# Two FFN f-tiles column by column, six late token tiles, and the token sums in the third f-tile

## The chip, the cores and the metric

One core of one Trainium2 chip runs the whole program in one launch. The metric is the device time of one execution in microseconds (us), the median of several runs. TensorE (PE) multiplies matrices and transposes, VectorE (DVE), ScalarE (ACT) and GpSimd (POOL) do the elementwise work, and SyncE (SP) issues nearly all DMA transfers, in the order of its queue.

## The reference

Two layers of a streaming encoder over 1024 prompt tokens and 8 x 16 sample tokens (1152 rows of 1024 channels, float32). Layer 0 mixes tokens with a gated recurrence and an attention, layer 1 with trailing pooling windows. Each mixer is followed by a layer norm, a convolutional FFN and another layer norm. The change touches the FFN's first half and the end of the mixers:

```
x = layer_norm(alpha * x + mixer(x))
a, b = split(x @ w_up)                 # w_up: 1024 x 5632, so a and b have 2816 columns each
c = conv_b + a[t-2]*cw[0] + a[t-1]*cw[1] + a[t]*cw[2]
f = (silu(c) * b) @ w_down
x = layer_norm(alpha * x + f)
```

## The kernel before

**Layout.** Tokens are held in nine tiles of 128 rows (`acc`, after the layer norm) and, transposed, as channels by tokens in `xh` and `xl`: each float32 value is split into a rounded high part and the rest, and every product is three matmuls (high x high, high x low, low x high; `mm3`, L145). `to_xt` (L201) transposes one token tile: twice four transpositions on PE into a PSUM bank, then `split`: ACT copies the high part into `xh`, DVE subtracts and writes `xl`. Weights come by DMA into a `raw` tile (three buffers) and are split in halves by `split_half` (L161): ACT writes `hi`, POOL writes `lo` (eight buffers each). `load_up` loads 128 columns of `w_up` and takes two of each.

**Before the FFN.** In layer 0 the output projection (L1170 on) adds its products tile by tile to `acc`, and `layer_norm` works on each: sums and small steps on DVE, square and scaling on ACT, the gain on DVE (POOL for tiles 4, 5 and 7), the bias on POOL (L232), then a store of the rows. Three tiles later (`LATE = 3`, L1178) the tile is transposed. In layer 1 the pooling mixer does the same (L1638). The last three tiles are `late`: they are transposed inside the FFN.

**The FFN's first half** (`ffn_up`, L1190) runs over 22 f-tiles of 128 columns of a and of b. The first three (`PLAIN = 3`) are plain: six products each, part a or b times a column of 384 tokens (`CHUNKS`), 24 matmuls a product. `put_a` (ACT) copies a into `ext`, DVE copies b into `bb` (two buffers each). `conv` (L1215) turns them into `cv`: a scaling on ACT, four multiply-adds on DVE (L1225), SiLU on ACT, two small copies on POOL, the product with `bb` on DVE (L1230), a DMA to `g_scr`. The other 19 f-tiles use a recombination with seven products of half the tokens and half the channels instead of eight (`SEVEN`); it needs sums of token halves (`t1`, `t2`, `t3`, and `t4`) and sums of weights (`prepare`, L1320). One such f-tile is 168 matmuls of 288 columns. The sums of weights use the temporaries `sa` and `sb`, one buffer each, that the token sums use too.

**The token sums** (`combine`, L1276) go by four channel pairs kk. Each takes three sums on POOL (L1281, L1282, L1291), five on DVE and the splits of t1, t2, t3 (ACT, DVE). The fourth sum is split into two `raw` buffers and written to `t4_scr` in DRAM; `swap` (L1299) reads it back over the part of `xh` and `xl` that is no longer needed, since the sixth product of every recombined f-tile takes it from there. `combine` stands beside the second and the third f-tile, two steps after each product of the second, one after each of the third; `swap` stands after the third.

**Order.** The program names for each operation its engine, and a planner orders every engine's queue by its own estimates: whatever is ready by these, earliest in the program first. So an operation can be moved ahead of others that stand earlier, and on the chip each queue is then worked off in that fixed order.

Of the kernel before, what the change touches and what calls it, by code (L numbers as in the profile page):

```python
# [25 lines left out]
NT = NTOK // 128  # L26
# [15 lines left out]
LEVELS = (1, 2, 4, 8, 16, 32, 64)  # L42
LAST = 3
LATE = 3

FAST = (6, 7, 8)
PG = (1, 2, 8)
# [63 lines left out]
def hybrid_stream_kernel(ctx: ExitStack, tc: tile.TileContext, i, o, k):  # L111
# [27 lines left out]
    def bank(shape, name):  # L139
        return ps.tile(shape, F32, tag="b", name=name)  # L140
# [4 lines left out]
    def mm3(out, ah, al, bh, bl, first, last):  # L145

        mm(out, ah, bh, first, False)
        mm(out, ah, bl, False, False)
        mm(out, al, bh, False, last)
# [10 lines left out]

    def split_half(src, sub=None):  # L161

        hi = wp.tile([128, 512], F32R, tag="wh", name="hi", bufs=8)
        lo = wp.tile([128, 512], F32R, tag="wl", name="lo", bufs=8)
        split(hi, lo, src, sub or nc.gpsimd)
        return hi, lo

# [33 lines left out]
    def to_xt(src, t0):  # L201
        for j in range(0, KD, 4):
            p = bank([128, 4, 128], "pxt")
            for q in range(4):
                tr(p[:, q, :], src[:, (j + q) * 128:(j + q + 1) * 128])
            split(xh[:, j:j + 4, t0:t0 + 128], xl[:, j:j + 4, t0:t0 + 128], p)
# [35 lines left out]
    def ln_apply():  # L242
        while ln_due:
            ln_due.pop(0)()
# [850 lines left out]
    with ExitStack() as ph:  # L1095
        so = pool_of(ph, "so", 2, side="right")
        rms_scale(ssa.rearrange("p t h -> p (t h)"), 128)

        def fetch(t):
            if t not in early:  # L1100
                ot = so.tile([128, 8, 128], F32, tag="ot", name="ot", bufs=3)
                load_heads(t, ot)
                early[t] = ot, gate(t, so.tile([128, H, 128], F32, tag="gate", name="gt"))

        def heads_norm(t):
            ot, gt = early.pop(t)
            for h in range(H):
                nc.vector.scalar_tensor_tensor(ot[:, h, :], ot[:, h, :], ssa[:, t, h:h + 1], gt[:, h, :],
                                               ALU.mult, ALU.mult)
            return ot.rearrange("t h c -> t (h c)")  # L1110

        y0 = [raw_tile("y0").rearrange("p (t c) -> p t c", c=256) for _ in range(2)]

        w1 = []

        def first_columns():

            ots = {}
            for t in range(NPT + 3):
                if t == 4:  # L1120
                    w1.append(load_cols(w_out, 256))
                if t < NPT:
                    fetch(t)
                if 1 <= t <= NPT:
                    ots[t - 1] = heads_norm(t - 1)
                    yield
                if 2 <= t < NPT + 2:
                    to_xt(ots.pop(t - 2), (t - 2) * 128)
                    yield
                if t >= 3:  # L1130
                    p = bank([128, 256], "po")
                    for _ in tm_unit(w0, t - 3, p):
                        yield
                    nc.scalar.copy(y0[(t - 3) // 4][:, (t - 3) % 4, :], p)
                    yield

        weave(first_columns(), running, R5)
        last_gate = gate(NPT, so.tile([128, H, 128], F32, tag="gate", name="gt"))
        drain(running)
        at_s.close()  # L1140
        acc = open_acc()
        load_acc(acc, x_rows)
        sp = pool_of(ph, "sp", 2, side="right")
        sums = sp.tile([128, NT, 4], F32, name="sums", bufs=1)

        def out_unit(w, t, j):
            p = bank([128, 256], "po")
            drain(tm_unit(w, t, p))
            add_res(acc[t], slice(256 * j, 256 * j + 256), p, sums[:, t, j:j + 1])

        last_ot = so.tile([128, 8, 128], F32, tag="ot", name="ot", bufs=3)
        load_heads(NPT, last_ot)
        early[NPT] = last_ot, last_gate
        last_ot = heads_norm(NPT)
        for t in range(NT):
            if t == 4:
                to_xt(last_ot, NPT * 128)
            if t == 6:
                out_unit(w0, NPT, 0)
                w2 = load_cols(w_out, 512)  # L1160
            out_unit(w1[0], t, 1)
            if t < NPT:
                add_res(acc[t], slice(0, 256), y0[t // 4][:, t % 4, :], sums[:, t, 0:1])
        w3 = load_cols(w_out, 768)
        g_bc = bcast(sp, i["ln1_g"][0], "g", "g_bc")
        b_bc = bcast(sp, i["ln1_b"][0], "bb", "b_bc")
        for t in range(3):
            out_unit(w2, t, 2)
        for t in range(NT):
            if t + 3 < NT:  # L1170
                out_unit(w2, t + 3, 2)
            if t + 3 == NT - 1:
                first = [load_up(0, 0, nc.vector), load_up(0, FF, nc.vector)]
            ln_apply()
            out_unit(w3, t, 3)
            nc.vector.tensor_tensor(sums[:, t, 0:2], sums[:, t, 0:2], sums[:, t, 2:4], ALU.add)
            layer_norm(sp, acc[t], sums[:, t], g_bc, b_bc, nc.gpsimd if t in OG else None, scr_rows(0, t))
            if t >= LATE:  # L1178
                to_xt(acc[t - LATE], (t - LATE) * 128)


    HALF = NTOK // 2
# [7 lines left out]
    def ffn_up(l, acc, late, first, leave):  # L1190
# [41 lines left out]
            yield  # L1232
            nc.sync.dma_start(g_scr[l][f], cv)

        def plain(f, w, order):

            _, _, bb = begin(f)
            for part, c in order:
                a, n = CHUNKS[c]
                p = bank([128, n], "pu")  # L1240
                for kk in range(KD):
                    mm3(p, w[part][0][kk], w[part][1][kk], xh[:, kk, a:a + n], xl[:, kk, a:a + n],
                        kk == 0, kk == KD - 1)
                if part == 0:
                    put_a(f, a, p, n)
                else:
                    nc.vector.tensor_copy(bb[:, a:a + n], p)
                yield


        u = plain(0, first, [(0, 0), (0, 1), (1, 0), (1, 1), (0, 2), (1, 2)])
        for s in range(6):
            next(u)
            if s == 0:
                ln_apply()
            if s == 1:
                store_rows()
            if s in (1, 2, 3) and late:
                t = late.pop(0)
                to_xt(acc[t], t * 128)  # L1260
            if s == 3:
                second = [load_up(l, 128), load_up(l, FF + 128)]
        drain(u)
        close_acc()

        tt_s = ExitStack()
# [9 lines left out]
        def combine(kk):  # L1276
# [13 lines left out]
            A, B = temp("sa"), temp("sb")  # L1290
            nc.gpsimd.tensor_tensor(A, xh[:, 4 + kk, h0], xl[:, 4 + kk, h0], ALU.add)  # L1291
            nc.vector.tensor_tensor(B, A, C, ALU.subtract)
            parts = [raw_tile("t4") for _ in range(2)]
            split(*[r[:, 0:HALF].bitcast(F32R) for r in parts], B)
            yield
            for n in range(2):
                nc.sync.dma_start(t4_scr[l][kk, n], parts[n][:, 0:HALF])

        def swap():  # L1299
            for n, x in enumerate((xh, xl)):  # L1300
# [36 lines left out]
                   "s3": b[:, up], "s4": a[:, lo]}[name]  # L1337
            wts[n] = [x.rearrange("p (k c) -> p k c", c=128) for x in split_half(src)]

        both = [(p, c) for p in range(2) for c in range(3)]  # L1340
        side = chain(*[combine(kk) for kk in range(4)])
        third = []
        for f, w in ((1, second), (2, third)):
            u = plain(f, w, both)
            cv = conv(f - 1)
            for s in range(6):
                next(u)
                if s in (0, 2):
                    next(cv, None)
                if f == 1 and s == 4:  # L1350
                    third += [load_up(l, 256), load_up(l, FF + 256)]
                if f == 2 and s in (1, 2):
                    fetch(PLAIN, s - 1)
                if f == 2 and s >= 4:
                    prepare(s - 4)
                for _ in range(2 if f == 1 else 1):
                    next(side, None)
            drain(u)
            drain(cv)
        drain(side)  # L1360
        swap()
        fetch(PLAIN + 1, 0)
        for n in range(2, AHEAD):
            prepare(n)

        banks = {}
# [3 lines left out]
        for n in range(n_last + 1):  # L1370
            f, m = PLAIN + n // 7, n % 7
            if m == 0:
                begin(f)
            prepare(n + AHEAD)
            if m == 0 and f + 1 < NF:
                fetch(f + 1, 1)
            if m == 2 and f + 2 < NF:
# [173 lines left out]
    def pool_mixer(acc, late, ws):  # L1551

        with ExitStack() as ph:
# [61 lines left out]
            for n in range(NT + 1):  # L1615
# [19 lines left out]
                    windows(0, [(band[:, 0], us[0])])  # L1635
                elif 1 < n <= NPT:
                    windows(n - 1, [(band[:, 1], us[n - 1]), (band[:, 2], us[n - 2])])
                if n > LATE:  # L1638
                    to_xt(acc[n - 1 - LATE], (n - 1 - LATE) * 128)
            windows(NPT, [(band_s[:, 0], us[NT]), (band_s[0:120, 1], us[NPT])])  # L1640
        return first

# [2 lines left out]
    def ahead_weights():  # L1645
        got["ws"] = load_pool_weights()

    acc = conv_ffn(0, False, acc, list(range(NT - LATE, NT)), first, ahead_weights)
    first = pool_mixer(acc, list(range(NT - LATE, NT)), got["ws"])
    conv_ffn(1, True, acc, list(range(NT - LATE, NT)), first)  # L1650


_INS = ["x_prompt", "x_sample", "cache_k", "cache_v", "state_hgrn", "state_pool", "state_ffn_conv",
# [30 lines left out]
```

## Time and profile before

| | us |
|---|---|
| median of 3 runs | 2605.75 |
| lowest, highest | 2600.84, 2606.06 |
| profiled execution, its own time | 2601.48 |
| span of the profiled execution | 2599.7 |

The profile shows one execution. Its page gives each engine's busy time; the trace behind it can be asked for waits (who waited, for which operation), for a timeline of single instructions, for groups of equal instructions and for busy times in a stretch. A matmul's duration includes its way through the array; the distance from one start to the next is what a matmul costs in a row of them. The granted clock is a share of TensorE's full 2.4 GHz.

The FFN of layer 0 begins at 900.1 us, that of layer 1 at 1782.9 with three matmuls and at 1786.1 without a break.

### The profile page before, as it was taken

The numbers are of one execution on the slowest core, as the hardware profiler recorded it, in microseconds if no ns is written. First come the engines' busy times: TensorE is split into PE (matmuls) and PEld (weight loads), VectorE is DVE, ScalarE is ACT, GpSimd is POOL, SyncE is SP. The second block draws the span as 40 slices with busy tenths as digits, with TensorE's granted clock in tenths as the row PEclk, the third lists the DMA queues.
The fourth block names the chain that finished last, engine by engine and source line by source line (L and its number), as shares of the span: only waits on it lengthen the run. The fifth ranks groups of instructions, "written<-read, shape, count | busy, mean of one in ns | idle before, by whom it ended". The sixth has DMA issues, their size and how long they took to land. (4 is left out here: it accounts for less than half of the span.)

```text
span 2599.7 us, 45443 instructions
## 1 busy us (share of the span) xinstructions
PE 2505.4 (96%) x18090; PEld 2301.7 (89%) x18090; DVE 1531.6 (59%) x2706; ACT 1074.1 (41%) x2176; POOL 967.1 (37%) x729
## 2 busy tenths in 40 slices
PE   8999999999999898999999999988899999999997
PEld 8999988786879898999999788878899999987886
DVE  3377754337884675554444665787655554556557
ACT  2255545354772433444444111265344444431113
POOL 1110111005652355555554122244555555531222
PEclk9999999998999999999999999999999999999999
DMA  5744247777666114222224422222332222252222
GB/s 169 203 113 125 83 158 241 237 249 226 235 219 233 66 70 135 71 77 77 77 77 150 141 95 78 76 80 75 118 102 70 73 73 77 77 210 90 95 78 82
DMA packets 279538, 323.78 MB, mean 125 GB/s; under 512 B 46379, under 2 KB 209780, under 8 KB 279327
## 3 DMA queue, kind: packets, MB, share of 16 engines
q1 hardware_dynamic: 276901, 319.26, 37.4%
q8 instruction: 142, 2.33, 0.4%
q10 hardware_dynamic: 2426, 1.63, 0.3%
q14 instruction: 69, 0.57, 0.1%
HBM read 244.38 MB, written 76.46 MB: 123 GB/s over the span
## 5 line engine op out<-in xcount | busy, mean ns | idle before, releaser
L156 POOL TENSOR_TENSOR lo<-raw,hi 128x512 fp32r<-128x512 f32 x362 | 531.6, 1481 | 1103.2 <-ACT hi L155 976.1
L143 PE MATMUL pu<-xh,lo 128*128 128x288 f32 (+1 forms) x1504 | 457.1, 304 | 7.7 <-POOL lo L156 7.7
L155 ACT CAST hi<-raw 128x512 fp32r<-128x512 f32 x378 | 230.1, 620 | 556.7 <-PE pu L143 283.0
L143 PE MATMUL pu<-xl,hi 128*128 128x288 f32 (+1 forms) x1504 | 456.5, 304 | 3.0 <-DVE xl L156 3.0
L143 PE MATMUL pu<-xh,hi 128*128 128x288 f32 (+1 forms) x1504 | 457.1, 304 | 1.0 <-ACT hi L155 0.5
L143 PE MATMUL pd<-lo,gh 128*128 128x512 f32 x792 | 315.2, 398 | 0.0
L143 PE MATMUL pd<-hi,gh 128*128 128x512 f32 x792 | 313.7, 396 | 0.0
L143 PE MATMUL pd<-hi,gl 128*128 128x512 f32 x792 | 310.4, 393 | 0.4 <-DVE gl L156 0.4
L143 PEld LDWEIGHTS pu<-xh,lo 128*128 128x128 f32 x1504 | 283.8, 189 | 9.0 <-POOL lo L156 9.0
L143 PEld LDWEIGHTS pu<-xl,hi 128*128 128x128 f32 x1504 | 284.2, 189 | 3.6 <-DVE xl L156 3.6
L143 PEld LDWEIGHTS pu<-xh,hi 128*128 128x128 f32 x1504 | 283.9, 189 | 2.1 <-ACT hi L155 1.2
L1452 DVE TENSOR_TENSOR acc<-acc,pd 128x512 f32<-128x512 f32 x330 | 216.3, 684 | 117.5 <-PE pd L143 117.2
L143 PE MATMUL ptm<-hi,xh 128*128 128x256 f32 x720 | 209.2, 291 | 3.9 <-ACT hi L155 3.9
L1225 DVE SCALAR_TENSOR_TENSOR cv<-ext,prm,cv 128x1024 f32<-128x1024 f32 (+1 forms) x176 | 183.8, 1099 | 34.8 <-ACT cv L1222 34.8
L143 PE MATMUL ptm<-lo,xh 128*128 128x256 f32 x720 | 201.8, 280 | 0.1
L143 PE MATMUL ptm<-hi,xl 128*128 128x256 f32 x720 | 201.6, 280 | 0.0
L143 PEld LDWEIGHTS pd<-hi,gh 128*128 128x128 f32 x792 | 148.7, 188 | 38.0 <-ACT gh L155 0.6
L143 PEld LDWEIGHTS pd<-hi,gl 128*128 128x128 f32 x792 | 148.5, 188 | 36.7 <-DVE gl L156 1.3
L143 PEld LDWEIGHTS pd<-lo,gh 128*128 128x128 f32 x792 | 148.7, 188 | 33.8
L143 PEld LDWEIGHTS ptm<-hi,xh 128*128 128x128 f32 x720 | 136.3, 189 | 7.1 <-ACT hi L155 4.3
L143 PEld LDWEIGHTS ptm<-lo,xh 128*128 128x128 f32 x720 | 136.3, 189 | 0.9 <-DVE lo L156 0.4
L143 PEld LDWEIGHTS ptm<-hi,xl 128*128 128x128 f32 x720 | 135.8, 189 | 0.0
(331 smaller groups left out, 5749.4 us busy)
## 6 DMA issues: line engine op xcount, KB each, us to landing
raw<-in_ffn_w_up SPq DMA_DIRECT2D x88, 512.0 KB
kraw<-in_cache_k SPq DMA_DIRECT2D x64, 512.0 KB
vraw<-in_cache_v SPq DMA_DIRECT2D x64, 512.0 KB
g_scr<-cv SPq DMA_DIRECT2D x44, 576.0 KB
graw<-g_scr SPq DMA_DIRECT2D x44, 576.0 KB
raw<-in_ffn_w_down SPq DMA_DIRECT2D x44, 512.0 KB
raw<-in_w_in_ab SPq DMA_DIRECT2D x28, 512.0 KB
x_scr<-acc SPq DMA_DIRECT2D x18, 512.0 KB
```

What stands on the lines that cost most here:

```text
L143: nc.tensor.matmul(out, a, b, start=start, stop=stop, skip_group_check=True)
L155: nc.scalar.copy(hi, src)
L156: (sub or nc.vector).tensor_tensor(lo, src, hi, ALU.subtract)
L1225: nc.vector.scalar_tensor_tensor(dst, tap[j], cw[j], dst, ALU.mult, ALU.add)
L1452: nc.vector.tensor_tensor(acc[t][:, cs], acc[t][:, cs], p, ALU.add)
```

## The change

`LATE_UP = 6`: before the FFN only tiles 0, 1 and 2 are transposed, six tiles after they were made, and the FFN gets six late tiles. (Between layer 0 and the pooling mixer it stays at three.) The first two f-tiles are done together: for each column of tokens the four products of both, with one late tile transposed after each of the second to eighth (the fifth left out). The weights of the second f-tile are loaded after two products, those of the third after all twelve. The convolution of the first f-tile begins in the last column. The token sums: two steps before the third f-tile, three after each of its products. The fourth sum is split in two halves of 288 tokens by `split_half`, so on POOL instead of DVE and into the buffers of the weights' parts instead of `raw`, and written by four DMAs instead of two. The first weights are prepared after the fourth product of the third f-tile, and `swap` stands in the third recombined product.

```diff
-            if t >= LATE:
-                to_xt(acc[t - LATE], (t - LATE) * 128)
+            if t >= LATE_UP:
+                to_xt(acc[t - LATE_UP], (t - LATE_UP) * 128)
...
-        u = plain(0, first, [(0, 0), (0, 1), (1, 0), (1, 1), (0, 2), (1, 2)])
-        for s in range(6):
-            next(u)
-            if s == 0:
-                ln_apply()
-            if s == 1:
+        begin(0)
+        begin(1)
+        for c in range(3):
+            for f, part in ((0, 0), (0, 1), (1, 0), (1, 1)):
+                if c == 0 and f == 1 and part == 0:
+                    second = [load_up(l, 128), load_up(l, FF + 128)]
+                plain(f, second if f else first, part, c)
+                if c == 0:
+                    ln_apply()
+                if c < 2 and (f, part) != (0, 0) and late:
+                    t = late.pop(0)
+                    to_xt(acc[t], t * 128)
+                if c == 2 and f:
+                    next(cv)
+            if c == 0:
                 store_rows()
-            if s in (1, 2, 3) and late:
-                t = late.pop(0)
-                to_xt(acc[t], t * 128)
-            if s == 3:
-                second = [load_up(l, 128), load_up(l, FF + 128)]
-        drain(u)
+            if c == 1:
+                cv = conv(0)
+        third = [load_up(l, 256), load_up(l, FF + 256)]
         close_acc()
...
-            parts = [raw_tile("t4") for _ in range(2)]
-            split(*[r[:, 0:HALF].bitcast(F32R) for r in parts], B)
+            for a in (0, HALF // 2):
+                cs = slice(a, a + HALF // 2)
+                parts = split_half(B[:, cs])
+                for n in range(2):
+                    nc.sync.dma_start(t4_scr[l][kk, n][:, cs], parts[n].bitcast(F32))
             yield
-            for n in range(2):
-                nc.sync.dma_start(t4_scr[l][kk, n], parts[n][:, 0:HALF])
...
-        third = []
-        for f, w in ((1, second), (2, third)):
-            u = plain(f, w, both)
-            cv = conv(f - 1)
-            for s in range(6):
-                next(u)
...
-                for _ in range(2 if f == 1 else 1):
-                    next(side, None)
+        for _ in range(2):
+            next(side)
+        cv = chain(cv, conv(1))
+        begin(2)
+        for s in range(6):
+            plain(2, third, s // 3, s % 3)
+            for _ in range(2 if s < 4 else 1):
+                next(cv, None)
+            if s in (0, 1):
+                fetch(PLAIN, s)
+            if s >= 3:
+                prepare(s - 3)
+            for _ in range(3):
+                next(side, None)
         drain(side)
-        swap()
+        drain(cv)
         fetch(PLAIN + 1, 0)
-        for n in range(2, AHEAD):
+        for n in range(3, AHEAD):
             prepare(n)
...
             prepare(n + AHEAD)
+            if n == 2:
+                swap()
...
-                if n > LATE:
-                    to_xt(acc[n - 1 - LATE], (n - 1 - LATE) * 128)
+                if n > LATE_UP:
+                    to_xt(acc[n - 1 - LATE_UP], (n - 1 - LATE_UP) * 128)
```

## Rows read from the trace of the kernel before

**Rows 1.** Page, first part: busy us (share of the span) and instructions by engine.
```profile
PE 2505.4 (96%) x18090; PEld 2301.7 (89%) x18090; DVE 1531.6 (59%) x2706; ACT 1074.1 (41%) x2176; POOL 967.1 (37%) x729
```

**Rows 2.** TensorE's waits, 887 to 1010: waiter <- releaser: total us, times, longest.
```profile
PE pu L143 <- ACT ext L1392: 8.3, 2, 7.1
PE pxt L152 <- POOL acc L232: 5.4, 2, 5.3
PE pu L143 <- POOL lo L156: 3.9, 2, 3.1
PE pu L143 <- DVE xl L156: 3.0, 2, 1.5
```

**Rows 3.** The same, 1786 to 1892 (layer 1): the longest.
```profile
PE pu L143 <- ACT ext L1392: 7.8, 2, 6.7
```

**Rows 4.** TensorE, one line's range, and timeline: start, us, engine, line, op, tiles, [idle before].
```profile
L143 PE MATMUL pu<-xh,hi x1504: 293/296/522, 900.1 to 2304.1; 128*128 128x288 f32 x152, 128*128 128x384 f32 x36
...
922.19 1.03 PE L152 MATMUL pxt<-ident,acc 128*128 128x128 f32 x8
923.46 0.79 PE L143 MATMUL pu<-xh,hi 128*128 128x384 f32 x3 [0.24 <-ACT xh L155]
...
1004.87 0.40 PE L143 MATMUL pu<-t2h,hi 128*128 128x288 f32 x1 [1.22 <-ACT ext L1392]
...
1786.08 0.34 PE L143 MATMUL pu<-xh,hi 128*128 128x384 f32 x1
...
1887.68 0.61 PE L143 MATMUL pu<-t2h,hi 128*128 128x288 f32 x1 [1.07 <-ACT ext L1392]
```

**Rows 5.** Stretches: from:to length, busy us (count) by engine, PEclk, DMA share, GB/s.
```profile
887.00:900.00 13.00, 7.56 (x46) 7.16 (x46) 8.79 (x19) 8.15 (x14) 9.47 (x4) 0.74 0.22 77
...
923.40:956.70 33.30, 33.24 (x192) 33.24 (x192) 25.90 (x33) 14.35 (x25) 16.25 (x13) 1.00 0.26 86
...
924.20:978.20 54.00, 49.88 (x285) 48.92 (x284) 43.05 (x53) 20.56 (x33) 29.45 (x20) 1.00 0.19 64
...
1006.00:1028.00 22.00, 22.00 (x168) 22.00 (x167) 11.69 (x18) 9.81 (x20) 13.29 (x10) 1.00 0.29 92
...
1887.60:1890.00 2.40, 2.32 (x9) 2.32 (x10) 2.23 (x1) 1.44 (x5) 2.40 (x2) 0.50 0.78 238
```

**Rows 6.** POOL by group, 924.2 to 978.2: busy us, mean ns of one, idle before.
```profile
L1291 POOL TENSOR_TENSOR sa<-xh,xl 128x576 f32<-128x576 f32 x4 | 7.2, 1807 | 11.5 <-DVE sc L1285 6.4 <-DVE t1l L156 5.0
...
L1281 POOL TENSOR_TENSOR sb<-xh,xl 128x576 f32<-128x576 f32 x4 | 6.7, 1677 | 9.9 <-DVE xl L156 5.2 <-DVE t L156 4.7
```

**Rows 7.** DVE by group, the same stretch.
```profile
L1225 DVE SCALAR_TENSOR_TENSOR cv<-ext,prm,cv 128x1024 f32<-128x1024 f32 x4 | 8.0, 2002 | 0.0
...
L1284 DVE TENSOR_TENSOR sb<-sc,sb 128x576 f32<-128x576 f32 x4 | 3.0, 756 | 0.2
...
L1230 DVE TENSOR_TENSOR cv<-cv,bb 128x1152 f32<-128x1152 f32 x1 | 1.4, 1350 | 0.0
```

**Rows 8.** Timeline, POOL and DVE, single operations of the sums.
```profile
939.25 1.43 POOL L1281 TENSOR_TENSOR sb<-xh,xl 128x576 f32<-128x576 f32 x1 [4.02 <-DVE t L156]
...
957.39 1.27 POOL L156 TENSOR_TENSOR lo<-raw,hi 128x512 fp32r<-128x512 f32 x1
...
957.46 1.81 DVE L1292 TENSOR_TENSOR sb<-sa,sc 128x576 f32<-128x576 f32 x1 [1.32 <-POOL sa L1291]
```

**Rows 9.** Timeline, DVE and POOL: splits of late tiles, layer norm of tile 8.
```profile
909.34 0.68 DVE L156 TENSOR_TENSOR xl<-pxt,xh 128x512 fp32r<-128x512 f32 x1
...
915.34 2.40 POOL L232 TENSOR_TENSOR acc<-acc,b_bc 128x1024 f32<-128x1024 f32 x1
...
923.44 1.29 DVE L156 TENSOR_TENSOR xl<-pxt,xh 128x512 fp32r<-128x512 f32 x2 [0.35 <-ACT xh L155]
```

**Rows 10.** Timeline, SP's queue.
```profile
980.80 16.11 SPq L1315 DMA_DIRECT2D raw<-in_ffn_w_up  x2
996.97 0.57 SPq L1301 DMA_DIRECT2D xl<-t_scr  x1
```

More of the change, by code (lines that the diff above doesn't have):

```diff
@@ L44 @@
 LATE = 3
+LATE_UP = 6
 FAST = (6, 7, 8)
@@ L161, in split_half @@
     def split_half(src, sub=None):
-        hi = wp.tile([128, 512], F32R, tag="wh", name="hi", bufs=8)
-        lo = wp.tile([128, 512], F32R, tag="wl", name="lo", bufs=8)
+        n = src.shape[1]
+        hi = wp.tile([128, 512], F32R, tag="wh", name="hi", bufs=8)[:, 0:n]
+        lo = wp.tile([128, 512], F32R, tag="wl", name="lo", bufs=8)[:, 0:n]
         split(hi, lo, src, sub or nc.gpsimd)
@@ L1233, in conv, with plain @@
             nc.sync.dma_start(g_scr[l][f], cv)
[L1235 to L1248, printed above, removed]
-        u = plain(0, first, [(0, 0), (0, 1), (1, 0), (1, 1), (0, 2), (1, 2)])
-        for s in range(6):
-            next(u)
-            if s == 0:
-                ln_apply()
-            if s == 1:
-                store_rows()
-            if s in (1, 2, 3) and late:
-                t = late.pop(0)
-                to_xt(acc[t], t * 128)
-            if s == 3:
-                second = [load_up(l, 128), load_up(l, FF + 128)]
-        drain(u)
+        def plain(f, w, part, c):
+            a, n = CHUNKS[c]
+            p = bank([128, n], "pu")
+            for kk in range(KD):
+                mm3(p, w[part][0][kk], w[part][1][kk], xh[:, kk, a:a + n], xl[:, kk, a:a + n],
+                    kk == 0, kk == KD - 1)
+            if part == 0:
+                put_a(f, a, p, n)
+            else:
+                nc.vector.tensor_copy(open_f[f][2][:, a:a + n], p)
+        begin(0)
[13 more added lines that the diff above has]
+            if c == 0:
+                store_rows()
+            if c == 1:
+                cv = conv(0)
+        third = [load_up(l, 256), load_up(l, FF + 256)]
         close_acc()
@@ L1338, in prepare @@
             wts[n] = [x.rearrange("p (k c) -> p k c", c=128) for x in split_half(src)]
-        both = [(p, c) for p in range(2) for c in range(3)]
         side = chain(*[combine(kk) for kk in range(4)])
-        third = []
-        for f, w in ((1, second), (2, third)):
-            u = plain(f, w, both)
-            cv = conv(f - 1)
-            for s in range(6):
-                next(u)
[L1348 to L1355, printed above, removed]
-                for _ in range(2 if f == 1 else 1):
-                    next(side, None)
-            drain(u)
-            drain(cv)
+        for _ in range(2):
[12 more added lines that the diff above has]
+                next(side, None)
         drain(side)
-        swap()
+        drain(cv)
         fetch(PLAIN + 1, 0)
-        for n in range(2, AHEAD):
+        for n in range(3, AHEAD):
             prepare(n)
@@ L1646, in ahead_weights @@
         got["ws"] = load_pool_weights()
-    acc = conv_ffn(0, False, acc, list(range(NT - LATE, NT)), first, ahead_weights)
+    acc = conv_ffn(0, False, acc, list(range(NT - LATE_UP, NT)), first, ahead_weights)
     first = pool_mixer(acc, list(range(NT - LATE, NT)), got["ws"])
-    conv_ffn(1, True, acc, list(range(NT - LATE, NT)), first)
+    conv_ffn(1, True, acc, list(range(NT - LATE_UP, NT)), first)
 _INS = ["x_prompt", "x_sample", "cache_k", "cache_v", "state_hgrn", "state_pool", "state_ffn_conv",
```

## The prediction, made before the changed kernel was run

> **What bounds the kernel now.** I read the page's first part, then TensorE's waits, then the timelines and busy times of the stretches around them. TensorE is busy for 2505.4 of 2599.7 us [rows 1], so outside its waits nothing else can cost time, and the change adds or removes no matrix product and no transposition: it moves them. What it can win or lose is TensorE's idle time and the half clock behind it, in the first three f-tiles of each layer's FFN and in the stage before. There, in layer 0, TensorE waits 5.4 us for GpSimd's layer-norm addition before a transposition (the long one 5.3), 3.0 for a late xl, 3.9 for the lo parts of the third f-tile's weights and 8.3 for ext, the copy that the third recombined product has to wait for [rows 2]; in layer 1 the lo parts cost the same again and ext 7.8 [rows 3]. After such a wait the clock is lower: 0.74 of full on average over the 13 us around the layer-norm wait, 0.50 behind the ext wait of layer 1 [rows 5], which is the 1.2 GHz level.
>
> All but the first and second have one cause, and the reader can see it in one stretch. From 924.2 to 978.2 the token sums are made: DVE is busy 43.05 us and POOL 29.45, together 72.5 in 54.0 [rows 5]. They don't overlap, they block each other: a lo on POOL that began at 957.39 and takes 1.27 let DVE's sum of 957.46 end only after 1.81, against 0.756 for its equals [rows 7, 8]; POOL's sums take 1.43 alone and 1.68 to 1.81 on average here [rows 6, 8]. For operations with two SBUF inputs the two engines are one, and this one is full for the 54 us.
>
> The Trainium skill says the same in "SBUF — State Buffer", Who interferes with whom: a DVE instruction with two SBUF inputs and a GpSimd instruction that reads SBUF exclude each other for the whole instruction. The rows agree (1.81 for 0.756), and it speaks against this change, which moves a split from DVE to GpSimd inside a full stretch. By the opposite view (two free engines) the sums would hide and the first rival's time would come out.
>
> **The change part by part.**
>
> *Six late tiles, layer 0.* The wait of 5.4 us before the transposition of tile 4 goes, with about 2 us of half clock, and three tiles' transpositions (0.8 us each: eight at 922.19, then the product can go) leave the stage. The first FFN product, at 900.1 before [rows 4], could start near 890. But now tile 2 is transposed last, directly before the first column that needs it, and its splits sit where tile 5's did: between layer-norm steps of ACT and DVE. Tile 5's last xl began at 909.34 [rows 9], 10 us after its transpositions, which stood directly before the 900.1. So the first product can't end before about 900, as if it had started at S = 896; bounds 890 and 900, and I take 896 because the layer-norm chain (tile 8's last addition on POOL runs from 915.34 [rows 9]) is bound by DVE and POOL, not by the products.
>
> *Column order.* Column 0 now has four products. One product is 24 matmuls; 192 took 33.3 us [rows 5], so 4.16 each and 33.3 for the eight products of columns 0 and 1. The 3.0 us for a late xl go, as tiles 3 to 5 are wanted 17 us later. A column boundary costs 0.5 us (transposition at 922.19, product at 923.46, of which 0.8 is the transposition [rows 4]); there is one more of them per layer. The second f-tile's weights are now wanted after two products instead of six. Their lo parts go through POOL between the layer-norm additions, which run to 917.7; wanted at about 905, I take W = 2 us of waiting, bounds 0 and 8. In layer 1 these additions are further along when the FFN starts, and I take 0.
>
> *When the sums can begin.* The sums need all tokens. The last xl splits run from 923.44 for 1.29 [rows 9], 2.5 us after tile 8's transpositions began. Tile 8 is now transposed after eight products and five other late tiles instead of four and two: S + 33.3 + 5 x 0.8 + 0.5 + W + 2.5 = S + 40.3 + W. Layer 0: 938.3, against 924.7 before. Layer 1: S was 1786.1 [rows 4], less 0.5 for three matmuls that ran ahead and 0.8 for transpositions that leave the pooling stage (they partly fill its own waits, so not all 2.4): 1825.3. I call this point A.
>
> *What DVE and POOL must do from A until the second recombined product (s3) can run.* Before, four channel pairs' sums, nearly two convolutions and the four lo of the third weights took 54.0. Now: the same 54.0; less 0.75 (the first sum can run before A); less 4 x 0.75, the fourth sum's lo on DVE; plus eight of these on POOL with 288 columns, 0.72 each by 1.27 for 512 and 1.43 for 576 [rows 8]: 5.8; plus the rest of the second convolution, 1.4 for its product with bb [rows 7]; plus the first weights' lo, 1.3; plus, for s3, whose two temporaries are those of the token sums, three sums of 0.75 and one lo: 3.5. Sum 62.2. Bounds: 57 if the second convolution falls behind the sums, 67 with gaps such as ACT's part of a split.
>
> *What TensorE has from A on.* It began column 2 1.3 us before A. Four products are 16.7, the third f-tile 25.0, the first recombined product 3.1 (168 matmuls take 22.0 [rows 5], 24 of them per product): s3 is wanted at A + 43.6. It waits 18.6 us. Then 3.1 for s3 and 1.5 for the half clock, so that the third recombined product (s2) starts at A + 66.9.
>
> *What goes.* The wait for the third weights (3.9 per layer) goes: they are loaded before the third f-tile, and their buffers are free after the second column-2 product. The late raw loads go too, as the fourth sum no longer takes raw's three buffers. Both only let TensorE arrive earlier at the sums. The fourth sum's write and the exchange (SP's two reads of t4, at 996.97 before [rows 10]) stand behind the last sum at about A + 60, wanted by the sixth product at A + 76: hidden, unless something is queued before them (third rival). The halved t4 writes are four per channel pair instead of two on SP's queue, which is idle there: no cost.
>
> *The sum.* Before, s2's second half ran from 1004.87 at full clock and from 1887.68 at half [rows 4, 5], which puts s2's start at 1003.4 and, with 0.9 of lost clock, 1887.0. After: 938.3 + 66.9 = 1005.2 and 1825.3 + 66.9 = 1892.2. That is 1.8 and 5.2 later, 7.0 in all. From there both kernels run the same products. Against the profiled execution's 2601.48 us: 2608.5. That execution lies at the low end of the runs shown (2600.84, 2605.75, 2606.06), so I set the sum on the middle of low and high, 2603.5: **2610 us**.
>
> **The rivals.**
>
> *The sums hide.* If DVE and POOL work beside each other and a channel pair's chain follows the products, s2 starts at A + 46.7: 985.0 and 1872.0, 33 us earlier in all, 2570. For it: the waits named go, and TensorE has 42 us of products beside the sums. Against it: 54.0 us for the same sums in the trace, with blocked operations.
>
> *An early start and an order that favours the sums.* S = 890 and W = 0 in layer 0, and the second convolution behind the sums (57 instead of 62): s2 at 992.2 and 1887.2, 11 us earlier, 2592. For it: the layer-norm wait of 5.4 us certainly goes, and each engine's order is set by a planner that may see this. Against: tile 2's splits in the layer-norm chain.
>
> *The exchange comes late.* On SP the read of the fifth f-tile's second weights may be queued before the two reads of t4; it waits for a raw buffer that the sixth weights' split frees, at about A + 70. Two reads of 1152 KB at the 238 GB/s of this stretch [rows 5] take 10 us, so t4 lands at A + 81 instead of before A + 76: 5 us more per layer, 2620, slower. It decides from the point where the exchange is issued later than A + 66. For it: before the change just such a read stood ahead of the exchange, for 16 us [rows 10]. Against: the exchange is now behind fewer loads.
>
> **How the numbers follow.** Forecast 0.46, sums hide 0.14, early start 0.22, exchange late 0.18. About 0.2% (5.2 us around 2605.75) is what a measurement of this kernel can tell from no change. Faster (under 2600.5): all of the first rival, 0.19 of the second, 0.03 of the forecast's lower end: 0.36. Within: 0.23 of the forecast and 0.03 of the second: 0.26. Slower: 0.20 of the forecast and 0.18: 0.38. The forecast's own range is 2600 to 2621 (S 890 to 900, W 0 to 8, 57 to 67); the range for 8 in 10 reaches down past the second rival and up past the third, 2586 to 2625, and leaves out most of the first.
>
> **What would show it.** Right: no wait of TensorE for a layer-norm addition at 890 and none for the third weights; tile 8's xl about 14 and 19 us later than before; one wait of some 15 to 20 us in each layer before the second recombined product, ended by POOL's lo or DVE; DVE and POOL adding up to the stretch. Wrong: sums that end less than 50 us after tile 8's xl, or a third f-tile followed by its first products without a wait.

## The result, and the profile after

The changed kernel takes 2622.76 us (median of 4 runs, 2620.02 to 2623.65) against 2605.69 for the kernel before, also 4 runs on the same chip: a ratio of 1.0068, 95% interval 1.0051 to 1.0085. It is slower by 0.7%. The profiled execution took 2620.02, its span 2618.2, which is 18.5 more than the span before. The forecast was 2610: the right side, the right place, and less than half of the size (7.0 us, where the spans differ by 18.5 and the medians by 17.1).

Line numbers in the changed file are up to 8 higher than before. Page, first part, answering to [rows 1]: TensorE's busy time has grown by 4.5 us, with the same number of instructions: some of them ran at a lower clock.

```profile
PE 2509.9 (96%) x18090; PEld 2304.4 (88%) x18090; DVE 1545.0 (59%) x2698; ACT 1075.4 (41%) x2184; POOL 967.9 (37%) x745
```

TensorE's waits in the changed kernel, first from 880 to 1020 (layer 0, to be held against [rows 2]), behind the dots from 1770 to 1910 (layer 1, [rows 3]): total us, times, longest.

```profile
PE pu L144 <- ACT hi L156: 14.8, 2, 9.4
PE pu L144 <- ACT xh L156: 10.8, 3, 10.3
PE pu L144 <- POOL lo L157: 3.5, 2, 3.0
...
PE pu L144 <- ACT hi L156: 13.8, 2, 8.3
PE pu L144 <- POOL lo L157: 3.5, 2, 3.0
```

The waits for the layer-norm addition, for the xl, for the third weights' lo and for ext are gone. In their place stand 10.3 us for tile 2's xh in layer 0 and, in both layers, some 18 us for the parts of recombined weights. TensorE's timeline shows where, in layer 0 (start, us, engine, line, what, idle before).

```profile
890.14 1.03 PE L153 MATMUL pxt<-ident,acc 128*128 128x128 f32 x8
901.50 1.01 PE L144 MATMUL pu<-xh,hi 128*128 128x384 f32 x2 [10.32 <-ACT xh L156]
...
989.98 0.61 PE L144 MATMUL pu<-xh,hi 128*128 128x288 f32 x1 [5.41 <-ACT hi L156]
993.85 0.61 PE L144 MATMUL pu<-xh,lo 128*128 128x288 f32 x1 [3.02 <-POOL lo L157]
...
1007.84 0.61 PE L144 MATMUL pu<-t3h,hi 128*128 128x288 f32 x1 [9.43 <-ACT hi L156]
...
1009.60 0.44 PE L144 MATMUL pu<-t3h,hi 128*128 128x288 f32 x1
...
1014.37 0.29 PE L144 MATMUL pu<-t2h,hi 128*128 128x288 f32 x1
```

The first product begins at 901.50, the first recombined product waits twice, s3 begins at 1007.84, and s2 at 1014.37. Until shortly before its end, s3's matmuls are 0.24 us apart, those of s2 behind it about 0.13. The kernel before began s2 earlier than the 1003.4 that the prediction gives:

```profile
1000.44 0.61 PE L143 MATMUL pu<-t2h,hi 128*128 128x288 f32 x1 [7.12 <-ACT ext L1392]
```

But there the first half of s2 ran with its matmuls 0.24 us apart, and the second waited again [rows 4]. 1003.4 is the start from which s2 at full clock would have ended at the same time, so 11.0 us are lost up to here. The busy times of three stretches of the changed kernel show s3's half clock (length, busy us by engine in the order of [rows 5], PEclk, DMA share, GB/s; the second is from the end of tile 8's last xl, point A, to s3).

```profile
901.50:905.00 3.50, 3.50 (x13) 3.40 (x14) 2.52 (x7) 3.09 (x5) 3.37 (x3) 0.53 0.37 150
...
943.90:1007.80 63.90, 46.09 (x259) 45.19 (x257) 49.17 (x57) 24.32 (x44) 39.19 (x31) 0.86 0.21 73
...
1007.80:1014.30 6.50, 5.96 (x24) 5.62 (x25) 4.32 (x5) 3.49 (x8) 6.43 (x5) 0.52 0.50 175
```

DVE and POOL together are "busy" for 88.4 us in 63.9. Two engines that run side by side could be that busy. Here much of it is not work: an instruction that stands blocked counts as busy. The timeline of DVE and POOL in the changed kernel shows one such place; the same three multiply-adds of the convolution took 2.75 us where POOL had nothing to do (they are shown below, in the run before_dve).

```profile
942.63 1.29 DVE L157 TENSOR_TENSOR xl<-pxt,xh 128x512 fp32r<-128x512 f32 x2 [0.50 <-ACT xh L156]
...
954.71 1.88 POOL L1287 TENSOR_TENSOR sc<-xh,xl 128x576 f32<-128x576 f32 x1
...
955.22 5.99 DVE L1227 SCALAR_TENSOR_TENSOR cv<-ext,prm,cv 128x1024 f32<-128x1024 f32 x3
...
956.55 3.58 POOL L157 TENSOR_TENSOR lo<-raw,hi 128x512 fp32r<-128x512 f32 x2
```

5.99 us for 2.75 of work, beside a sum of 1.88 for 1.43 and two lo of 1.27 that took 3.58. Over the whole stretch I put each duration against that of the same instruction unblocked: by this estimate some 22 of the 88.4 us are standing still, and the 66 that are left are about as long as the stretch. At least one of the two engines is busy in 62.4 of the 63.9 us. The Trainium skill ("SBUF — State Buffer", Who interferes with whom) adds that the issue order decides which of the two engines blocks. The row agrees as far as it goes, since here both were held up in turn.

### The profile page after: what moved, and what is told of

Read it like the earlier page. It is cut to its first block, busy times and chain, and to the rows that moved or that the text cites. A ratio compares the mean times of both kernels' runs of the same rounds, so it can differ in the third digit from the quotient of the medians.

```text
span 2618.2 us, 45508 instructions
## 1 busy us (share of the span) xinstructions
PE 2509.9 (96%) x18090; PEld 2304.4 (88%) x18090; DVE 1545.0 (59%) x2698; ACT 1075.4 (41%) x2184; POOL 967.9 (37%) x745
## 5 line engine op out<-in xcount | busy, mean ns | idle before, releaser
L157 POOL TENSOR_TENSOR lo<-raw,hi 128x512 fp32r<-128x512 f32 x362 | 515.0, 1436 | 1077.7 <-ACT hi L156 951.6
```

The costliest lines, as they stand in the source:

```text
L157: (sub or nc.vector).tensor_tensor(lo, src, hi, ALU.subtract)
```

## The experiments

Every time is the median of its runs, every ratio that of its runs to runs of the kernel before on the same chip (2604.5 to 2605.9), with its 95% interval. Point A and the start of s3 are read from the timelines of DVE and TensorE.

| run | us | ratio | A, layer 0 | s3 begins | A to s3, layer 0 and 1 |
|---|---|---|---|---|---|
| the change | 2622.8 | 1.0068 | 943.9 | 1007.8 | 63.9, 63.9 |
| early3 | 2625.3 | 1.0078 | 943.9 | 1007.8 | 63.9, 63.9 |
| early_t8 | 2609.4 | 1.0017 | 933.8 | 997.7 | 63.9, 63.9 |
| late3 | 2603.3 | 0.9999 | 925.5 | 997.7 | 72.2, 72.2 |
| no_taps | 2607.2 | one run | 943.1 | 997.7 | 54.6, 54.6 |
| dve_sums | 2603.2 | 0.9993 | 942.4 | 998.8 | 56.4, 56.5 |
| early_t8_dve | 2596.6 | 0.9970 | 939.4 | 995.7 | 56.3, 56.3 |
| late3_dve | 2587.1 | 0.9933 | 924.5 | 988.5 | 63.9, 64.6 |

My theory was that A plus a fixed length of work on two engines that exclude each other sets s3, whatever TensorE does. The rivals: DVE and POOL run side by side and something else is late; the sums are a chain of operations that wait for each other, with free engines in between; or A's place doesn't matter.

### Fewer late tiles: late3

```diff
-LATE_UP = 6
+LATE_UP = 3
```

> The changed kernel with three late tiles instead of six (LATE_UP = 3), all else as changed: tile 8 is transposed after four products instead of eight. My theory (DVE and POOL are one resource for the token sums, which take about 62 us from tile 8's last xl to the second recombined product): tile 8's last xl comes some 18 us earlier than in the changed kernel in each layer, the second recombined product starts 64 us after it as before, and the kernel takes about 2590 us, 33 less than the changed one and faster than the kernel before. Rival (the delay comes from the order of the loads and splits, whatever the start of the sums): 2615 to 2623.

Measured: 2603.32 us, ratio 0.9999 (0.9990 to 1.0009). The six late tiles are what makes the change slow: without them the rest of it costs nothing that can be told. But the 2590 that I expected were missed by 13 us. A came 18.4 us earlier, as expected, and s3 only 10.2, since the stretch behind A grew to 72 us. DVE and POOL did not get more to do: at least one of them is busy in 63.1 of these 72.2 us, against 62.4 of 63.9 in the change. Why 8 us more stand empty is the subject of the last four runs.

### The sums on DVE: dve_sums

```diff
-            nc.gpsimd.tensor_tensor(B, xh[:, kk, h1], xl[:, kk, h1], ALU.add)
-            nc.gpsimd.tensor_tensor(C, xh[:, 4 + kk, h1], xl[:, 4 + kk, h1], ALU.add)
+            nc.vector.tensor_tensor(B, xh[:, kk, h1], xl[:, kk, h1], ALU.add)
+            nc.vector.tensor_tensor(C, xh[:, 4 + kk, h1], xl[:, 4 + kk, h1], ALU.add)
...
-            nc.gpsimd.tensor_tensor(A, xh[:, 4 + kk, h0], xl[:, 4 + kk, h0], ALU.add)
+            nc.vector.tensor_tensor(A, xh[:, 4 + kk, h0], xl[:, 4 + kk, h0], ALU.add)
```

> The changed kernel with POOL's three token sums of each channel pair on DVE. My theory (operations with two SBUF inputs of the two engines exclude each other): twelve operations of 1.43 us become twelve of 0.75 in the same sequence, the 62 us from tile 8's xl to the second recombined product become about 54 in each layer, 2606 us in all. Rival (the engines work beside each other and DVE is the longer one): DVE gets 9 us more per layer, 2640 us.

Measured: 2603.23 us, ratio 0.9993 (0.9983 to 1.0002), 19.5 us under the change. Twelve sums more on the engine that was already the busier one, and the stretch is 7.5 us shorter. Its row, from A to s3 in layer 0 of dve_sums, has DVE at 52.98 of 56.30: now one engine is full, by work. The waits of TensorE from 940 to 1030 in the same run follow it.

```profile
942.40:998.70 56.30, 46.82 (x259) 45.92 (x257) 52.98 (x71) 25.12 (x46) 21.66 (x19) 0.91 0.24 82
```

```profile
PE pu L144 <- ACT hi L156: 7.1, 2, 6.5
PE pu L144 <- POOL lo L157: 2.4, 1, 2.4
PE pu L144 <- DMA xl<-t_scr: 0.9, 1, 0.9
```

9.5 us for hi and lo instead of 18.3. Side by side, DVE's stretch should have grown by what it was given; the rival of 2640 is out. A chain of operations that wait for each other would get shorter by this edit too, since each sum is shorter on DVE; no_taps tests that.

### The first three tiles as early as before: early3

```diff
-            if t >= LATE_UP:
-                to_xt(acc[t - LATE_UP], (t - LATE_UP) * 128)
+            if 3 <= t < 6:
+                to_xt(acc[t - 3], (t - 3) * 128)
```

(and the same in the pooling mixer)

> The changed kernel with tiles 0 to 2 transposed three tiles after they were made, as in the kernel before; tiles 3 to 8 stay late. My theory (the first FFN product of layer 0 waits 10.3 us for tile 2's split, which stands between layer-norm steps): this wait goes, tile 8's xl in layer 0 comes about 8 us earlier, layer 1 stays: 2613 us. Rival (the layer-norm chain holds up tiles 3 to 8 as well): the wait moves to the next transposition or product, 2621 us.

Measured: 2625.3 us, ratio 1.0078 (1.0062 to 1.0095), no faster than the change (in layer 1, which was to stay, A came at 1839.9 against 1835.4). My theory missed. TensorE's timeline in early3, layer 0:

```profile
890.27 0.34 PE L144 MATMUL pu<-xh,hi 128*128 128x384 f32 x1
...
900.44 0.44 PE L144 MATMUL pu<-xh,hi 128*128 128x384 f32 x1 [0.81 <-ACT hi L156]
904.71 0.66 PE L144 MATMUL pu<-xh,lo 128*128 128x384 f32 x1 [3.65 <-POOL lo L157]
...
913.18 0.45 PE L144 MATMUL pu<-xh,lo 128*128 128x384 f32 x1 [1.57 <-POOL lo L157]
...
920.13 0.62 PE L144 MATMUL pu<-xh,hi 128*128 128x384 f32 x2 [1.74 <-ACT xh L156]
922.20 0.69 PE L144 MATMUL pu<-xl,hi 128*128 128x384 f32 x1 [1.02 <-DVE xl L157]
```

The first product does begin at 890.27, 11.2 us earlier. Then TensorE waits for the second f-tile's hi and lo and for later tiles' splits, 8.8 us and the half clock behind them, and tile 8's last xl ends at 943.9 as in the change. So the 11.2 us were given back: with tile 2's late split out of the way, the weights' parts on POOL and the later tiles' parts on ACT and DVE hold the products up instead.

### Tile 8 two products earlier: early_t8, early_t8_dve

```diff
-                if c < 2 and (f, part) != (0, 0) and late:
+                step = 4 * c + 2 * f + part
+                for _ in range({1: 1, 2: 1, 3: 2, 4: 1, 5: 1}.get(step, 0)):
```

(early3's edit stands too; early_t8_dve has the sums of dve_sums and the fourth sum's lo parts on DVE)

> The changed kernel with tiles 0 to 2 transposed as early as in the kernel before and the six late tiles put after products one to five, so that tile 8 is transposed after six products instead of eight; sums as in the change. My theory (the stretch from tile 8's last xl to the second recombined product is 64 us whatever lies ahead of it): tile 8's last xl ends two products, 8.3 us, earlier than 943.9, near 935.5, the third recombined product starts near 1006, and the time falls by 8 us per layer from the 2625 of the early tiles alone: 2609 (2605 to 2614). Rival: the layer norm of the late tiles and the first weights' lo parts, which TensorE already waited for with early tiles, set when tile 8 can come: A stays at 941 to 944 and the time at 2620 to 2626.

> The same order of tiles, with GpSimd's three token sums and the fourth sum's lo parts on DVE. My theory: tile 8's last xl near 935.5 and 56 us from there to the second recombined product (as the sums on DVE showed), so that product starts near 992, about 16 us earlier than in the changed kernel, with a wait of 2 to 5 us left, in both layers: 2590 (2586 to 2597). Rival: tile 8 doesn't come earlier (2602 to 2606, as with the sums on DVE alone).

Measured: 2609.36 us, ratio 1.0017 (1.0008 to 1.0027), and 2596.63, ratio 0.9970 (0.9958 to 0.9982). Two products fewer ahead of tile 8 bring A to 933.8, and s3 follows 63.9 us behind; with the sums on DVE at 56.3. TensorE's timeline, early_t8:

```profile
997.70 0.61 PE L144 MATMUL pu<-t3h,hi 128*128 128x288 f32 x1 [7.73 <-ACT hi L156]
```

The second missed its middle (2590) by 6.6 us, because its layer 0 began later: its first product stands at 894.2 against 888.6 in early_t8, and A 5.6 later with it. Why that part moved is open, but single executions differ by as much: the profiled one of early_t8 was the fastest of its ten (2605.11), that of early_t8_dve the second slowest of its six (2598.72), and the first product began anywhere from 900.1 to 905.8 in the kernel before and the runs with three late tiles.

### Without the taps: no_taps

```diff
-                for j in (1, 2):
+                for j in (1, 2) if f > 1 else ():
```

> The changed kernel without the multiply-adds of the convolution (second and third tap) in the first two f-tiles, so part of the computation is left out; they aren't in the chain of the token sums. My theory (DVE and POOL exclude each other and are full): about 6 us of DVE per layer less, the time from tile 8's xl to the second recombined product falls from 64 to about 57, 2609 us. Rival (the sums are a chain of dependences through the single buffers of their temporaries, about 10 us for each channel pair, and the engines are free in between): 64 us stay 64, 2620 us.

Measured in one run: 2607.24 us. Four multiply-adds less in each of two f-tiles, on DVE only, and s3 comes 9.3 us sooner behind A, in both layers. The ones left out make some 6 of it. Another 2.3 come from the third f-tile's taps: 3.1 us of them stood ahead of s3 in the change, 0.8 here. 1 us is left over. The chain of sums has no tap in it and should have kept its 64 us, so that rival is out; the stretch is made of both engines' work. Its row in no_taps:

```profile
943.10:997.70 54.60, 45.65 (x260) 45.18 (x258) 36.32 (x45) 24.07 (x44) 37.59 (x31) 0.93 0.25 85
```

### The kernel before with its sums on DVE: before_dve, and late3_dve

before_dve is the kernel before with the edit of dve_sums alone; late3_dve is late3 with it and with the fourth sum's lo on DVE.

> The kernel before, with GpSimd's three token sums per channel pair on DVE and nothing else changed. My theory: DVE and GpSimd block each other in the kernel before too, so its sums end earlier and the wait for ext (8.3 us in layer 0, 7.8 in layer 1) shrinks by 6 to 8 us per layer: 2592 (2588 to 2597). Rival: in the kernel before the ext wait is set by ACT's copies and the products, not by the sums' engines, and DVE only gets longer: 2604 to 2612.

> The changed kernel with three late tiles instead of six, the three token sums that GpSimd made and the fourth sum's lo parts on DVE. My theory: with three late tiles tile 8's last xl ends near 925 (as with three late tiles alone), and with the sums on one engine the stretch from there to the second recombined product loses about 8 us, so the wait of 7.7 us before that product goes in both layers and its half clock with it: two times 8 to 9 us less than the 2603.3 of three late tiles alone, 2586 (2583 to 2592), under the kernel before. Rival: the two gains are the same gain (both only shorten one wait of which less than half was left), or DVE, now busy nearly all of the stretch, becomes the late engine: 2598 to 2604.

Measured: 2574.10 us, ratio 0.9883 (0.9868 to 0.9897), and 2587.09, ratio 0.9933 (0.9918 to 0.9948). late3_dve came within its range. before_dve went the way of its theory, but gained more than I gave it and lies 14 us below its range: the kernel before loses 30.6 us by three changed engine names (2604.66 on the same chip). TensorE's one wait from 930 to 1010 in before_dve, against 8.3 for ext and 3.9 for lo before [rows 2], and DVE's taps in the same run with an idle POOL beside them:

```profile
PE pu L143 <- ACT ext L1392: 1.0, 1, 1.0
```

```profile
931.80 2.75 DVE L1225 SCALAR_TENSOR_TENSOR cv<-ext,prm,cv 128x1024 f32<-128x1024 f32 x3
```

I had counted the ext wait only; the 3.9 us per layer for the third weights' lo (POOL, now free) went too. With 1.0 and 1.3 us of ext's wait left, these waits make 21.6 of the 30.6 us. The half clock behind them is part of the rest, which is not worked out here.

### The 8 us behind A: late3_order, late3_dve_order, raw_dve, raw_pool

In late3 the stretch from A was 72 us, in late3_dve 64, each 8 longer than theory. ACT's and DVE's timelines in late3 show a hole from 936 on; I put it down to the third weights' hi, which waits for a buffer.

```profile
942.60 0.62 ACT L156 CAST hi<-raw 128x512 fp32r<-128x512 f32 x1 [5.59 <-PE pu L144]
```

```diff
-        third = [load_up(l, 256), load_up(l, FF + 256)]
...
-        for _ in range(2):
+        for _ in range(6):
             next(side)
+        third = [load_up(l, 256), load_up(l, FF + 256)]
```

> Three late tiles (as late3), and two whole channel pairs' sums put ahead of the third f-tile's weights instead of two thirds of one; engines of the sums as in the change. With three late tiles alone ACT's split of the third weights waits until 942.60 for TensorE to give the first weights' buffers free, and ACT's t1h, t2h, t3h of the second pair stand behind it, so DVE and GpSimd make no sums from 936 to 943 and the stretch from tile 8's last xl to the second recombined product is 72 us instead of 64. My theory: put ahead, the sums fill this hole, the stretch becomes 64 again, TensorE hardly waits before that product, and the time falls by about 8 us per layer to 2587 (2583 to 2594). Rival: the hole is not the order but the products that the convolution waits for; the same sums then only trade places and the time stays at 2600 to 2604.

> The same order, with GpSimd's three token sums and the fourth sum's lo parts on DVE (late3_dve with the two pairs ahead of the third weights). My theory: the wait of 4.7 us before the second recombined product and the half clock behind it go in both layers: 2574 (2569 to 2580), as fast as the kernel before with its sums on DVE (2574.1). Rival: TensorE is already at its products and another wait takes the place: 2583 to 2588.

Measured: 2605.07 us, ratio 0.9998 (0.9989 to 1.0008), and 2586.79, ratio 0.9930 (0.9915 to 0.9945): nothing gained. My reading was wrong, and ACT's timeline in late3_order says what it had been:

```profile
943.93 0.43 ACT L156 CAST hi<-sb 128x288 fp32r<-128x288 f32 x1 [5.58 <-PE pu L144]
```

The third weights are no longer in front, and another hi waits as long for the same release: that of the fourth sum. The change puts its parts into the eight buffers of the weights' parts, and these hold the first two f-tiles until column 2 has read them. So the fourth sum of the first channel pair stands, and the second pair behind it. One more edit takes it out of these buffers:

```diff
-                parts = split_half(B[:, cs], nc.vector)
+                r = raw_tile("t4").bitcast(F32R)
+                parts = [r[:, 0:HALF // 2], r[:, 512:512 + HALF // 2]]
+                split(*parts, B[:, cs], nc.vector)
```

> late3_dve_order with one more edit: the two parts of the fourth sum are made in a raw buffer instead of two of the eight weight buffers. There the hole stayed: ACT's hi of the fourth sum stood from 937 to 943.6 behind TensorE, since the eight weight buffers hold the first two f-tiles until column 2 has read them, and everything of the second channel pair is queued behind that hi. My theory: with raw buffers the second pair's sums fill the hole, the stretch from tile 8's last xl to the end of the sums is about 8 us shorter, and the waits before and in the first recombined products (1.4 and 2.3 us, with half clock) go in both layers: 2576 (2570 to 2581). Rival: the raw buffers are late in the same way, behind the weights' loads, or TensorE's waits are set by something else: 2584 to 2590.

> The same order and the same raw buffers with the sums' engines as in the change (GpSimd makes three sums and the fourth sum's lo parts). My theory: with the hole filled the port-bound stretch of 64 us from 925.5 ends near 990, TensorE's waits there shrink to 0 to 3 us: 2588 (2583 to 2594). Rival: 2600 to 2606, no change against late3_order.

Measured: 2574.42 us, ratio 0.9879 (0.9863 to 0.9895), and 2596.16, ratio 0.9961 (0.9947 to 0.9975). In raw_dve the fourth sum's two hi stand at 936.81 on ACT, the sums run on, and TensorE is busy from 930 to 985 without a gap, DVE for 95% of it. ACT's timeline of raw_dve, then its stretch:

```profile
936.81 0.77 ACT L156 CAST t<-sb 128x288 fp32r<-128x288 f32 x2 [1.99 <-DVE sb L1296]
```

```profile
930.00:985.00 55.00, 55.00 (x320) 55.00 (x319) 52.39 (x75) 24.78 (x45) 11.80 (x12) 1.00 0.31 103
```

raw_pool gained 8.9 us where I expected 17 (2588, range to 2594). Its hole is filled as well, but with the sums ahead the convolutions end later, and TensorE waits 3.1 us for the third weights' lo and 6.5 for ext, much as in the kernel before (TensorE's waits in raw_pool, 922 to 1010):

```profile
PE pu L144 <- ACT ext L1398: 6.5, 1, 6.5
PE pu L144 <- POOL lo L157: 3.4, 2, 3.1
```

With the sums still on POOL, the order has only chosen which wait is the long one. before_dve and raw_dve are the fastest kernels of the study, 1.2% under the kernel before, and equal to each other: once the sums are on DVE, the rest of the change wins nothing over the kernel before.

## Why the prediction was right, and where it fell short

**The cause.** Right: the token sums are work of two engines that exclude each other. dve_sums and no_taps each change one side and the stretch follows; in before_dve TensorE's waits go. The first rival (the sums hide, 2570) is out.

**62.2 us from A to s3.** 63.9 were measured in both layers and, with A moved by ten, 63.9 again. Off by 1.7.

**What goes.** The layer-norm wait, the wait for late xl, for the third weights and for ext went, as said. TensorE waits some 18 us per layer for the sums (18.6 predicted; 5.4, 3.0 and 9.4 in layer 0), but in three places: I had not seen that the first recombined weights' split is queued behind token sums too. This changes nothing in the end, since s3 is the later one.

**S, the step that failed.** The start of the first product was put at 896 with 900 as upper bound; it came at 901.50. I had the cause (tile 2's split between layer-norm steps of ACT and DVE) and still chose the middle, although tile 2's place in the layer norm spoke for the upper end. (In dve_sums and no_taps, the same program up to there, it came at 899.7 and 899.8.) W = 2 us was to be a wait for the second weights' lo; there was none. Behind the long wait the clock was 0.53 for 3.5 us, 1.6 of loss, which took its place. So A was 943.9 for 938.3: 5.6 us of the miss.

**Half clock.** After s3's wait I allowed 1.5 us for it. s3 ran at 0.52 on average and took 6.5 us instead of 4.6: 1.9. With the 1.7 above and S this is layer 0's whole miss: s2 came 11.0 us later than before where 1.8 was predicted, and 5.6 + 1.7 + 1.9 = 9.2. What the sum left out comes behind s2: at 1028.37 TensorE waits 1.0 us for DVE to read bb, and in the next f-tile the products stand 12.4 us later than before.

**Layer 1.** A should have come at 1825.3 (the prediction's own terms add up to 1825.1). It came at 1835.4, or 1823.0 without layer 0's 12.4, so 2.3 early. The stretch and s3 took 1.7 and 1.6 more than reckoned, so s2, at 1905.6, is 1.0 late without layer 0's share. In the next f-tile the products stand 18.9 us later than before, 6.5 of it layer 1's own, where 5.2 were predicted. The spans differ by 18.5.

**The range.** The measured 2622.76 lies outside the forecast's own range, 2600 to 2621, though the bounds of S, W and the stretch, all at their late ends, would have allowed some 2630. It lies inside 2586 to 2625 because that range was stretched to hold the third rival, which cost next to nothing: that part was luck.

**The rivals.** The early start (S = 890, W = 0, 2592) had a term that exists, as early3 shows, but S and W are not independent: with S at 890.27 the weights and the tiles are late by what was won. The late exchange (2620) is near the measured time, but not by its mechanism. SP's timeline in the changed kernel, then its wait from 1006 to 1014.7:

```profile
1006.48 0.37 SPq L1307 DMA_DIRECT2D xh<-t_scr  x1
1014.61 0.38 SPq L1321 DMA_DIRECT2D raw<-in_ffn_w_up  x1
1015.10 0.52 SPq L1307 DMA_DIRECT2D xl<-t_scr  x1
...
SPq L1321 <- POOL lo L157: 7.4, 1, 7.4
```

A read of weights did stand ahead of the second of the two reads and held it for 7.4 us, so it was issued later than the mark A + 66 = 1009.9. But the read of xh had gone before, and the sixth product came at A + 80 instead of A + 76. TensorE waits 0.3 us for xl in layer 1 and not at all in layer 0, where 5 were reckoned per layer.

**Not seen at all.** The fourth sum's parts in the weights' buffers, which I counted as a gain because raw's buffers come free. In the change itself, whose A lies behind column 2's start, its stretch shows no such hole: ACT waits there for no buffer that TensorE has to give free. With three late tiles and the sums ahead of the third weights it costs what late3_dve_order and raw_dve differ by, 12.4 us.

## What to carry to other kernels

Where two engines exclude each other, add their work up to one line and ask when it can start and what waits for its end; a sum moved to the fuller engine can then be a gain, if it runs shorter there (0.75 us on DVE for 1.43 on POOL). Before delaying the input of such a line by a rearrangement upstream, see whether the line is already on the path. And a temporary that is put into a pool of buffers shared with weights waits for the weights' last reader, together with everything queued behind it.

## Not expected

The stretch behind A kept its length to 0.1 us between layers and runs with six late tiles, although A itself moved by ten. And "busy" overstated the work of two blocked engines by some 22 us in 63.9 here (the estimate above), so busy times don't tell work from blocking; an instruction's duration against that of its unblocked equals does.
